# The expert loop of a hybrid S5/SSD/MoE block: scatter and gather moved ahead of each expert's branch

## The chip, the core and the metric

The kernel runs on one core of one Trainium2 chip. The metric is the device time of one execution in microseconds (us); the kernel before takes 1868.61 us, the median of 3 runs (1868.11 to 1870.3). A core has five engines that run side by side, each with an instruction queue of its own: TensorE (PE, matrix products; its weight loads are a row of their own, PEld), VectorE (DVE), ScalarE (ACT), GpSimd (POOL) and SyncE (SP, which here only issues the loads of weights). Weights come from HBM by DMA, through 16 DMA engines.

## What is computed

The reference is one layer: a modulated RMS norm, a projection, an S5 mixer and an SSD mixer, a merge, and then a mixture of experts, which is the second half of the time and all that the change touches. For 256 tokens of width 1024 it is, cut to its core:

```python
logits = (xf @ p['router_w'] + p['router_b']).astype(jnp.float32)
top_val, top_idx = lax.top_k(logits, TOP_K)            # 4 of 32 experts per token
gates = jax.nn.softmax(top_val, axis=-1)
...
def expert_block(args):
    tokens, e = args
    xb = x_pad[tokens]
    gate = jnp.minimum(xb @ p['moe_w_gate'][e] + p['moe_b_gate'][e], SWIGLU_LIMIT)
    up = jnp.clip(xb @ p['moe_w_up'][e] + p['moe_b_up'][e], -SWIGLU_LIMIT, SWIGLU_LIMIT)
    act = (up + 1.0) * gate * jax.nn.sigmoid(SWIGLU_ALPHA * gate)
    return act @ p['moe_w_down'][e] + p['moe_b_down'][e]
...
y = y.reshape(n_slots, d) * slot_gate[:, None].astype(y.dtype)
return jax.ops.segment_sum(y, slot_token, num_segments=n + 1)[:n].reshape(b_, l, d)
```

All weights are float32: three matrices of 1024 x 1024 per expert, 12 MB, for 32 experts.

## The kernel before

**The expert loop** (line 1711) walks experts 0 to 31 in pairs: an even one (j = 0) and the odd one behind it (j = 1). Each expert has room for 64 tokens (CAP). A pair shares one 128-column gather, one slot table and one result tile.

**One expert, in program order.** `load.until` (L1774) issues on SP the loads of weight tiles of 1 MB, four each for gate, up and down. `count` (L1694) reads the expert's token count into registers of PE, ACT and DVE. `before.scale` (L1595) multiplies the last expert's result by its gates on DVE. `inner` does the gate and the up product on PE (both L1502), and `swiglu` (L1506 to L1510) on DVE and ACT, which ends in tile `au`. `beyond` (L1677) is a branch that PE, ACT and DVE take when the expert has more than 64 tokens: it runs a second, smaller pass over the same three weight matrices. The branch bounds the scheduling: no instruction crosses it. Behind it stand, for an even expert, the scatter of the last pair (`scatter`, L1601 on PE and L1603 on DVE: four matmuls of 128x512, each added to `h2`), for an odd one the gather of the next pair (`Pair`, 48 matmuls at L1532, two copies at L1535, one-hot tables at L1518). Then comes `outer`: four transposes of `au` (L1575), their copy `aT` (L1577), for an even expert the pair's slot table (`slots`, L1545 to L1554), and the down product (L1588). The last expert has four warming matmuls (L305) behind its branch.

**What sets the order.** The order on each engine inside a stretch between two branches is chosen by a scheduler. In the profile the end of a branch is line L1681 on the engine's queue (PEq, DVEq); it is there whether or not the branch was taken.

**Buffers.** There are 17 weight tiles of 1 MB (`NBW = 12, 5`), 12 for one expert. The second pass reads gate and up again, so their eight tiles come free only when PE has passed the branch; the four of down come free as the down product reads them. SP's loads go round eight semaphores, so a load also waits until the one eight places before it has landed.

```python
    for e in range(NE):
        this = pair
        load.until(e + 1, sum(NBW))
        ...
        behind = this.inner(e % 2)
        beyond(e, n, levels, T)
        ...
        this.outer(e % 2)
```

Of the kernel before, what the change touches and what calls it, by code (L numbers as in the profile page):

```python
# [49 lines left out]
def build(tc, I, out):  # L50
# [1262 lines left out]
    M = es.enter_context(tc.tile_pool(name="moe", bufs=1, reuse_waits="tile"))  # L1313
    experts.more = es.enter_context(tc.tile_pool(name="moew2", bufs=NBW[1], reuse_waits="tile"))
    moe(tc, I, out, M, ident, epsc, gf, h2, xp, iot, posm, pos3, gate, cnt, first, oneh, bst, experts, warm)
    es.close()

# [163 lines left out]
def moe(tc, I, out, M, ident, epsc, gf, h2, xp, iot, posm, pos3, gate, cnt, first, oneh, bst, load, warm):  # L1481
# [5 lines left out]
    def pst(tag, bufs):  # L1487
        return ps.tile([P, 512], F32, tag=tag, name="p_" + tag, bufs=bufs)
# [23 lines left out]
    class Pair:  # L1512
# [54 lines left out]
            self.u = u_  # L1567
            return mm, *swiglu(pg, pu, g_, s_, u_)

        def outer(self, j):  # L1570
            e = self.e0 + j
            u_ = self.u
            pa = pst("t", 2)
            for q in range(4):
                pe.transpose(pa[:, q * P:(q + 1) * P], u_[:, q * P:(q + 1) * P], ident)  # L1575
            aT = M.tile([P, 4, 2, CAP], F32, tag="aT", name="aT")
            act.copy(aT.rearrange("p a b s -> p (a b s)"), pa)  # L1577
            if j == 0:
                self.slots()
            py = pst("y", 2)  # L1580

            for q in range(2):
                pe.matmul(py[64 * q:64 * q + 64], oneh[:, e:e + 1].to_broadcast([96, CAP]), bst[2][:, 512 * (q ^ j):512 * (q ^ j) + 512],
                          start=True, stop=False)
            for k in range(KD):
                for q in range(2):
                    c = k * D + 512 * (q ^ j)
                    self.done = pe.matmul(py[64 * q:64 * q + 64], aT[:, k % 4, k // 4], wts[e, 2, c // load.unit][:, c % load.unit:c % load.unit + 512],  # L1588
                              start=False, stop=(k == KD - 1))
            self.py = py  # L1590
# [53 lines left out]
    def extra_out(e, c, T):  # L1644

        nq = P // c
        n = D // nq
        nb = n // P
        ST, u_ = T.sb("oST", 256), T.sb("oxu", 512)
        pa = T.ps("t1", "t", 2)  # L1650
        for b in range(nb):
            pe.transpose(pa[:, b * P:(b + 1) * P], u_[:, b * P:(b + 1) * P], ident)
        aT = T.sb("oaT", 512)[:, 0:n]
        act.copy(aT, pa[:, 0:n])
        aT = aT.rearrange("p (b q s) -> p b q s", b=nb, q=nq)
        py = T.ps("t0", "t", 2)
        gemm(py, e, 2, lambda k: aT[:, k % nb, k // nb], c)
        ys = u_[:, 0:n]
        for q in range(nq):
            o = slice(c * q, c * q + c)  # L1660
            dve.tensor_mul(ys[o], py[o, 0:n], gf[o, n * q:n * q + n])
        per = 512 // n
        banks = [T.ps(*b, 2) for b in (("sc0", "sc"), ("sc1", "sc"), ("t1", "t"), ("t0", "t"))]
        for t0 in range(0, 2, per):
            for t in range(t0, t0 + per):
                for q in range(nq):
                    o = slice(c * q, c * q + c)
                    pe.matmul(banks[t0 * nq + q][:, (t - t0) * n:(t - t0 + 1) * n], ST[o, t * P:(t + 1) * P], ys[o], start=True, stop=True)
            for q in range(nq):
                ya = h2[:, t0:t0 + per, n * q:n * q + n]  # L1670
                dve.tensor_add(ya, ya, banks[t0 * nq + q].rearrange("p (t n) -> p t n", t=per))
# [3 lines left out]
    levels = (CAP, 32), (96, 32), (128, 64), (192, 64)  # L1675

    def beyond(e, n, rest, T):  # L1677

        if rest:
            base, c = rest[0]  # L1680
            with tc.If(n > base, label=f"more{e}" if base == CAP and e else None):  # L1681
                extra_in(e, base, c, T)
                extra_out(e, c, T)
                beyond(e, n, rest[1:], T)

    pair = Pair(0)
    last = before = None
    behind = []

    def count(e):  # L1690

        block = nc.cur_bb.bb.instructions
        start = len(block)
        n = nc.values_load(cnt[0:1, e:e + 1], engines=engs, min_val=0, max_val=NTOK)  # L1694
        for ins in block[start:]:
            for b in behind:
                if ins.engine == b.ins.engine:
                    tc.add_manual_dep(ins, b.ins.name, mybir.DependencyInfo(mybir.DependencyClass.NoSync, mybir.DependencyReason.DATA),
                                      reason="order")
        return n  # L1700

    def hint(e, after):

        block = nc.cur_bb.bb.instructions
        start = len(block)
        tc.mark_branch_hint_location(f"more{e}", "LikelyTaken", engines=[ET.PE])
        for ins in block[start:]:
            tc.add_manual_dep(ins, after.ins.name, mybir.DependencyInfo(mybir.DependencyClass.NoSync, mybir.DependencyReason.DATA),
                              reason="order")
# [4 lines that stand above are left out]
        if e == 0:  # L1714
            behind = this.through
        n = count(e)
        T = Shared(M, pst)
        if before:
            before.scale(1 - e % 2)

            hint(e, before.done)
        before = this
        behind = this.inner(e % 2)

        beyond(e, n, levels, T)
        if e % 2 == 0 and last:
            for t in range(2):
                last.scatter(t)
        if e % 2 and e + 1 < NE:
            last, pair = pair, Pair(e + 1)  # L1730
        if e == NE - 1:
            warm(WARM, pst("sc", 2))
        this.outer(e % 2)
    this.scale(1)

    ss = M.tile([P, 2, 2], F32, name="oss")
# [128 lines left out]
```

## Time and profile before

| | before |
|---|---|
| median of 3 runs | 1868.61 us (1868.11 to 1870.3) |
| the profiled execution | 1875.09 us, span 1873.4 us |
| mean granted TensorE clock | 0.934 |
| PE, DVE, ACT busy over the span | 86%, 46%, 25% |
| bytes moved by DMA | 539.54 MB |

The profile is one execution. Times are us from the first instruction; a row of the timeline gives the start, the duration and the instruction, and in brackets how long the engine sat idle before it and who ended that. A matmul of float32 operands shows as two passes in the trace. The expert loop starts near 864 us and holds the rest of the span. Experts 17 and 29 have more than 64 tokens and take the branch once.

### The profile page before, as it was taken

The numbers are of one execution on the slowest core, as the hardware profiler recorded it, in microseconds if no ns is written. First come the engines' busy times: TensorE is split into PE (matmuls) and PEld (weight loads), VectorE is DVE, ScalarE is ACT, GpSimd is POOL, SyncE is SP. The second block draws the span as 40 slices with busy tenths as digits, with TensorE's granted clock in tenths as the row PEclk, the third lists the DMA queues.
The fourth block names the chain that finished last, engine by engine and source line by source line (L and its number), as shares of the span: only waits on it lengthen the run. The fifth ranks groups of instructions, "written<-read, shape, count | busy, mean of one in ns | idle before, by whom it ended". The sixth has DMA issues, their size and how long they took to land. (4 is left out here: it accounts for less than half of the span.)

```text
span 1873.4 us, 28065 instructions
## 1 busy us (share of the span) xinstructions
PE 1616.0 (86%) x11244; PEld 1090.9 (58%) x11244; DVE 869.6 (46%) x1614; ACT 460.2 (25%) x796; POOL 291.1 (16%) x299
## 2 busy tenths in 40 slices
PE   5788888976978799797988989899898998989887
PEld 3566666764766698684555555445445554555443
DVE  6767799888997546754122221222122122221222
ACT  5333453542525565242000000000000000000001
POOL 5133435535432331200000000000000000000000
PEclk8899899888987899897999999999999999999999
DMA  8578545344532357684999999999978999999873
GB/s 300 174 235 239 172 140 140 114 123 113 151 114 63 112 184 264 208 273 188 420 419 421 419 420 419 419 419 420 420 319 366 409 419 419 419 420 420 366 317 146
DMA packets 141458, 539.54 MB, mean 288 GB/s; under 512 B 31752, under 2 KB 44968, under 8 KB 91968
## 3 DMA queue, kind: packets, MB, share of 16 engines
q1 hardware_dynamic: 136032, 526.95, 74.3%
q10 hardware_dynamic: 4656, 8.21, 1.3%
q8 instruction: 138, 2.26, 0.5%
q0 software_dynamic: 560, 1.52, 0.3%
q14 instruction: 72, 0.59, 0.1%
HBM read 529.86 MB, written 6.77 MB: 286 GB/s over the span
## 5 line engine op out<-in xcount | busy, mean ns | idle before, releaser
L1502 PE MATMUL p_gu<-mw,xe 128*64 128x512 f32 x2048 | 475.0, 594 | 5.2 <-DMA mw<-in_mg 3.9
L1502 PEld LDWEIGHTS p_gu<-mw,xe 128*64 128x64 f32 x2048 | 261.9, 137 | 181.6 <-issue 46.5
L1430 PE MATMUL mm<-uh,h 128*128 128x256 f32 (+1 forms) x1152 | 327.9, 364 | 44.5 <-DVE cv L1430 32.0
L1430 PEld LDWEIGHTS mm<-uh,h 128*128 128x128 f32 x1152 | 213.5, 205 | 84.2 <-issue 44.9
L1588 PE MATMUL p_y<-mw,aT 128*64 128x512 f32 x1024 | 236.4, 604 | 0.7 <-ACT aT L1577 0.7
L1430 PE MATMUL mm<-ul,h 128*128 128x256 f32 (+1 forms) x576 | 205.5, 357 | 0.0
L1430 POOL TENSOR_TENSOR h<-w,h 128x512 fp32r<-128x512 f32 x99 | 147.3, 1492 | 285.5 <-ACT h L1430 228.7
L1595 DVE SCALAR_TENSOR_TENSOR ye<-p_y,gs,xq 64x512 f32<-64x512 f32 x64 | 48.0, 750 | 256.8 <-PE p_y L1588 256.3
L1588 PEld LDWEIGHTS p_y<-mw,aT 128*64 128x64 f32 x1024 | 96.2, 139 | 118.5 <-issue 79.5
L1507 ACT ACTIVATE as<-ag 128x512 f32<-128x512 f32 (+1 forms) x34 | 21.0, 617 | 496.3 <-DVE ag L1506 496.3
L1430 ACT CAST h<-w 128x512 fp32r<-128x512 f32 x144 | 88.2, 618 | 164.6 <-PE mm L1430 118.7
L1430 PEld LDWEIGHTS mm<-ul,h 128*128 128x128 f32 x576 | 118.1, 205 | 13.4 <-issue 3.0
L1508 DVE TENSOR_SCALAR au<-p_gu 128x512 f32<-128x512 f32 x32 | 22.1, 692 | 205.7 <-PE p_gu L1502 205.7
L1506 DVE TENSOR_SCALAR ag<-p_gu 128x512 f32<-128x512 f32 (+1 forms) x34 | 23.0, 676 | 185.7 <-PE p_gu L1502 110.4
L1601 PE MATMUL p_sc<-ye,ST 128*128 128x512 f32 x128 | 69.3, 684 | 39.7 <-DVEq L1681 38.8
L1430 DVE SCALAR_TENSOR_TENSOR cv<-mm,cw,cv 128x508 f32<-128x508 f32 (+3 forms) x128 | 85.6, 673 | 12.4 <-ACT cv L1430 12.1
L1532 PE MATMUL p_t<-Sb,xp 128*128 128x128 bf16 x480 | 52.9, 250 | 36.0 <-DVEq L1681 36.0
L355 DVE TENSOR_TENSOR low<-w,hi 128x512 fp32r<-128x512 f32 x80 | 63.4, 800 | 34.9 <-ACT hi L353 34.0
L1430 ACT ACT_TABLE_LOAD x55 | 70.6, 1283 | 32.1 <-DVE cv L1430 31.3
L1601 PEld LDWEIGHTS p_sc<-ye,ST 128*128 128x128 f32 x128 | 23.5, 207 | 85.4 <-issue 62.4
L1577 ACT COPY aT<-p_t 128x512 f32<-128x512 f32 x32 | 18.7, 585 | 221.5 <-PE p_t L1575 221.5
L1532 PEld LDWEIGHTS <-xp 128*128 128x128 bf16 x512 | 43.0, 116 | 48.7 <-issue 40.4
(427 smaller groups left out, 2352.0 us busy)
## 6 DMA issues: line engine op xcount, KB each, us to landing
mw<-in_mg SPq DMA_DIRECT2D x128, 1024.0 KB
mw<-in_mu SPq DMA_DIRECT2D x128, 1024.0 KB
mw<-in_md SPq DMA_DIRECT2D x128, 1024.0 KB
w<-in_wg SPq DMA_DIRECT2D x96, 256.0 KB
ada<-in_ada SPq DMA_DIRECT2D x32, 256.0 KB
Toe<-in_ada SPq DMA_DIRECT2D x16, 512.0 KB
vT<-Ed SPq DMA_DIRECT2D x16, 512.0 KB
l8a<-in_ada SPq DMA_DIRECT2D x16, 512.0 KB
```

Source lines behind the costliest of these rows:

```text
L355: lo.tensor_tensor(low, w, hi.bitcast(F32), op=ALU.subtract)
L1430: return fn(*args, **kw)
L1502: mm = pe.matmul(dst[c * q:c * q + c, 0:n], lhs(k), w[:, o:o + n], start=False, stop=(k == KD - 1))
L1506: dve.tensor_scalar(g_, pg, 7.0, None, op0=ALU.min)
L1507: sg = act.activation(s_, g_, AF.Sigmoid, scale=1.702)
L1508: dve.tensor_scalar(u_, pu, -7.0, 7.0, op0=ALU.max, op1=ALU.min)
L1532: mm = pe.matmul(pt[:, k * P:(k + 1) * P], x[:, t, (k0 + k) * P:(k0 + k + 1) * P], Sb[:, t].rearrange("p j s -> p (j s)"), start=(n == 0), ...
L1577: act.copy(aT.rearrange("p a b s -> p (a b s)"), pa)
L1588: self.done = pe.matmul(py[64 * q:64 * q + 64], aT[:, k % 4, k // 4], wts[e, 2, c // load.unit][:, c % load.unit:c % load.unit + 512], sta ...
L1595: dve.scalar_tensor_tensor(self.y[rows, nh], self.py[rows], self.gs[rows, nh, j:j + 1], gf[rows, 512 * nh:512 * nh + 512], op0=ALU.mult, o ...
L1601: pe.matmul(pc, self.ST[:, nh, t], self.y[:, nh], start=True, stop=True)
```

## The change

The four steps behind the branch are spread around it. For an even expert, `scatter(0)` (the first two of the four matmuls of the last pair's scatter) is written ahead of the branch, and `scatter(1)` (the other two) moves into `outer`, behind the transposes and the slot table. For an odd expert, the whole gather of the next pair is written ahead of the branch. The last expert's warming matmuls are written ahead of its branch too. Nothing is computed that was not before, and nothing is left out.

```diff
-        def outer(self, j):
+        def outer(self, j, other=None):
...
             if j == 0:
                 self.slots()
+            if other:
+                other.scatter(1)
             py = pst("y", 2)
...
-        beyond(e, n, levels, T)
         if e % 2 == 0 and last:
-            for t in range(2):
-                last.scatter(t)
+            last.scatter(0)
         if e % 2 and e + 1 < NE:
             last, pair = pair, Pair(e + 1)
         if e == NE - 1:
             warm(WARM, pst("sc", 2))
-        this.outer(e % 2)
+
+        beyond(e, n, levels, T)
+        this.outer(e % 2, last if e % 2 == 0 else None)
```

What the scheduler makes of it on PE, around the branch of the even expert 30 (`mw,xe` are gate and up, `ye,ST` the scatter, `mw,aT` down). Before, the stretch ends in the up product, and all four matmuls of the scatter stand first behind the branch:

```order
L1502 MATMUL p_gu<-mw,xe 64x512 x4
L1694 TENSOR_LOAD cnt
L1694 ISA x2
L1681 COMPARE_AND_BRANCH
...
L1681 UNCONDITIONAL_BRANCH x5
L1601 MATMUL p_sc<-ye,ST 128x512 x4
L1575 MATMUL p_t<-ident,au 128x128 x4
L1545 MATMUL p_t<-ident,S 128x128 x4
...
L1551 MATMUL p_t<-gate,S 128x2 x4
L1588 MATMUL p_y<-mw,aT 64x512 x16
```

And now, at the same place:

```order
L1603 MATMUL p_sc<-ye,ST 128x512
L1502 MATMUL p_gu<-mw,xe 64x512 x4
L1603 MATMUL p_sc<-ye,ST 128x512
L1502 MATMUL p_gu<-mw,xe 64x512 x4
...
L1683 COMPARE_AND_BRANCH
...
L1683 UNCONDITIONAL_BRANCH x5
L1575 MATMUL p_t<-ident,au 128x128 x4
L1545 MATMUL p_t<-ident,S 128x128 x4
L1551 MATMUL p_t<-gate,S 128x2 x4
L1603 MATMUL p_sc<-ye,ST 128x512 x2
L1590 MATMUL p_y<-mw,aT 64x512 x16
```

The two early scatter matmuls do not stand between the up product and the branch: the scheduler has put them inside the up product, between its weight tiles (four matmuls each). What stands between the up product and the transposes is nothing but the branch.

On PE around the branch of the odd expert 29 (`Sb,xp` and `Sb,xq` are the gather). Before, the up product ends, the branch follows, and the gather's 48 matmuls are first behind it:

```order
L1502 MATMUL p_gu<-mw,xe 64x512 x16
L1694 TENSOR_LOAD cnt
...
L1681 COMPARE_AND_BRANCH
...
L1681 UNCONDITIONAL_BRANCH x5
L1532 LDWEIGHTS xp
L1532 MATMUL p_t<-Sb,xp 128x128
```

And now:

```order
L1532 MATMUL p_t<-Sb,xq 128x128
L1696 TENSOR_LOAD cnt
...
L1683 COMPARE_AND_BRANCH
...
L1683 UNCONDITIONAL_BRANCH x5
L1575 MATMUL p_t<-ident,au 128x128 x4
```

The gather now ends just ahead of the branch: 11 of its matmuls stand ahead of the up product's last four, 37 behind them. The transposes are first behind the branch.

On DVE around the branch of the odd expert 17, whose pair still builds a one-hot table `Sb` for a later gather. Before:

```order
L1510 TENSOR_TENSOR au<-au,as 128x512
L1694 TENSOR_LOAD cnt
L1681 COMPARE_AND_BRANCH
L1614 TENSOR_SCALAR oS<-iot,posm 128x32 x2
...
L1681 UNCONDITIONAL_BRANCH x5
L1518 TENSOR_TENSOR Sb<-iot,pos_8798 128x256
```

And now:

```order
L1510 TENSOR_TENSOR au<-au,as 128x512
L1518 TENSOR_TENSOR Sb<-iot,pos_8798 128x256
L1696 TENSOR_LOAD cnt
L1683 COMPARE_AND_BRANCH
L1616 TENSOR_SCALAR oS<-iot,posm 128x32 x2
```

The table moved ahead of the branch, behind the last step of swiglu; it overwrites the table that the gather reads. Experts 27 and later build none. The last expert's four warming matmuls moved, on PE, from the first place behind its branch to the last place ahead of it.

## Rows read from the trace of the kernel before

**Rows 1.** The page: busy tenths and GB/s in 40 slices of 46.8 us.
```profile
PE   5788888976978799797988989899898998989887
DMA  8578545344532357684999999999978999999873
GB/s 300 174 235 239 172 140 140 114 123 113 151 114 63 112 184 264 208 273 188 420 419 421 419 420 419 419 419 420 420 319 366 409 419 419 419 420 420 366 317 146
```
**Rows 2.** Waits of PE, 880 to 1873 us: total us, times, longest.
```profile
PE p_sc L1601 <- DVEq L1681: 38.8, 15, 2.7
PE p_t L1532 <- DVEq L1681: 36.0, 15, 2.5
...
PE p_gu L1502 <- DMA mw<-in_mg: 3.9, 1, 3.9
```
**Rows 3.** Timeline of PE, DVE and ACT, experts 15 and 16: start, duration, instruction, idle before.
```profile
1321.80 0.69 DVE L1508 TENSOR_SCALAR au<-p_gu 128x512 f32<-128x512 f32 x1 [6.32 <-PE p_gu L1502]
...
1324.40 0.38 PE L1532 MATMUL p_t<-Sb,xp 128*128 128x128 bf16 x4 [2.42 <-DVEq L1681]
...
1327.07 0.61 PE L1575 MATMUL p_t<-ident,au 128*128 128x128 f32 x4
...
1327.77 0.58 ACT L1577 COPY aT<-p_t 128x512 f32<-128x512 f32 x1
1331.90 1.11 PE L1502 MATMUL p_gu<-mw,xe 128*64 128x512 f32 x1 [3.89 <-DMA mw<-in_mg]
...
1353.92 1.94 PE L1502 MATMUL p_gu<-mw,xe 128*64 128x512 f32 x8
```
**Rows 4.** Timeline of SP: the first of four loads, time over the four issues.
```profile
1371.68 7.77 SPq L1774 DMA_DIRECT2D mw<-in_mg  x4
1381.62 29.75 SPq L1774 DMA_DIRECT2D mw<-in_mu  x4
1411.46 2.04 SPq L1774 DMA_DIRECT2D mw<-in_md  x4
...
1504.37 7.83 SPq L1774 DMA_DIRECT2D mw<-in_mg  x4
...
1717.84 7.83 SPq L1774 DMA_DIRECT2D mw<-in_mg  x4
```
**Rows 5.** Timeline of DVE and PE, experts 17 and 18, around the taken branch.
```profile
1385.62 0.69 DVE L1508 TENSOR_SCALAR au<-p_gu 128x512 f32<-128x512 f32 x1 [6.32 <-PE p_gu L1502]
...
1388.04 0.76 PE L1623 MATMUL p_t<-xp,oS 128*32 128x256 bf16 x16 [2.03 <-DVE oS L1614]
...
1438.65 0.69 DVE L1508 TENSOR_SCALAR au<-p_gu 128x512 f32<-128x512 f32 x1 [6.56 <-PE p_gu L1502]
```
**Rows 6.** One stage of 20 us: PE, PEld, DVE, ACT, POOL busy, clock, DMA share, GB/s.
```profile
1460.00:1480.00 20.00, 17.57 (x122) 11.56 (x120) 3.19 (x5) 2.30 (x4) 0.00 (x0) 1.00 0.97 393
```
**Rows 7.** Timeline of DVE and PE, experts 28 to 31.
```profile
1735.19 0.69 DVE L1508 TENSOR_SCALAR au<-p_gu 128x512 f32<-128x512 f32 x1 [6.56 <-PE p_gu L1502]
...
1765.11 0.69 DVE L1508 TENSOR_SCALAR au<-p_gu 128x512 f32<-128x512 f32 x1 [6.32 <-PE p_gu L1502]
...
1788.51 0.59 PE L1532 MATMUL p_t<-Sb,xp 128*128 128x128 bf16 x4 [2.31 <-DVEq L1681]
...
1792.46 0.61 PE L1575 MATMUL p_t<-ident,au 128*128 128x128 f32 x4
1794.10 7.03 PE L1588 MATMUL p_y<-mw,aT 128*64 128x512 f32 x32
...
1817.11 5.37 PE L1601 MATMUL p_sc<-ye,ST 128*128 128x512 f32 x8 [2.66 <-DVEq L1681]
...
1822.32 0.60 PE L1575 MATMUL p_t<-ident,au 128*128 128x128 f32 x4
...
1848.54 3.07 PE L305 MATMUL p_sc<-triUL,ident 128*128 128x256 f32 x8 [2.65 <-DVEq L1681]
1851.40 1.06 PE L1575 MATMUL p_t<-ident,au 128*128 128x128 f32 x4
```

## The prediction

> **What bounds the kernel now.** I read the page's slices first, then PE's waits, then the timeline around single branches, then SP's own timeline. In the slices [rows 1] the expert loop is the right half: the DMA engines are full and move 419 to 420 GB/s, and PE is busy 8 to 9 tenths as well. Two dents stand in the stream of weights, slices 30 to 32 (319, 366, 409 GB/s) and 38 to 39 (366, 317); they follow the two taken branches, of experts 17 and 29. Behind the second one the stream has ended before the program does (146 GB/s in the last slice). So two limits lie close together, and the question for any saving on PE is whether it is ahead of the stream or behind it.
>
> PE's waits [rows 2] answer half of it: its large waits are for the end of the branch on DVE, 38.8 us in 15 scatters and 36.0 us in 15 gathers, 2.4 to 2.6 us each. For weights it waited once for long, 3.9 us at expert 16. Everywhere else in the loop the weights were there before PE came.
>
> How far ahead they were is read from SP. Loads go round eight semaphores, so the fourth gate load of expert e+1 is issued when the last up tile of expert e has landed. For expert 17 that is 1371.68 + 7.77 - 0.33 (one issue, an estimate from four issues within 2.04) = 1379.1 us [rows 4]; the up product's last tile takes 1.94 us [rows 3], so PE could have been through at 1381.1. It was through at 1385.62, where DVE starts on its result [rows 5]: 4.5 us late. For expert 28 the same sum gives 1717.84 + 7.83 - 0.33 + 1.94 = 1727.3 [rows 4] against 1735.19 [rows 7]: 7.9 late. The stream's pace is (1717.84 - 1504.37) / 7 = 30.5 us per expert [rows 4], PE's (1735.19 - 1438.65) / 10 = 29.65 [rows 5, 7]. So PE catches up 0.85 us per expert, reaches the stream at expert 16 (the wait of 3.9 us), loses it in the branch of expert 17 and has not reached it again at 29. Between the branches, PE's time counts only as far as its lag reaches; behind the branch of 29 PE alone counts.
>
> **The change, part by part.** *Odd experts.* At expert 15 the result of the up product reaches DVE at 1321.80, the gather starts at 1324.40 after 2.42 us of idling, the transposes at 1327.07, the copy aT at 1327.77: 5.97 us in all [rows 3]. 48 gather matmuls took 1327.07 - 1324.40 = 2.67 us. After the change 37 of them (2.06 us) run while swiglu runs, 11 (0.61) ahead of the last up tile. DVE still has to pass the branch, now with the table Sb behind the gather: Sb needs the gather's end (about 2.1), then half a microsecond and the branch's own 0.4 or so; I put the transposes at 3.2 us and aT at 3.9. Saved: 5.97 - 3.9 - 0.61 = 1.4 us per odd expert.
>
> *Even experts.* The scheduler put the two early scatter matmuls inside the up product, not behind it, so the idle stretch of 2.66 us stays. The scatter took 1817.11 to 1822.32, 5.2 us, at expert 30 [rows 7]. Sixteen matmuls of the down product, two side by side, take 7.03 us [rows 7], 0.88 a pair, so I price a full-width one of the same columns at 0.88: four are 3.5 us wherever they stand. Saved: 1.7 us where the scatter ran at the lower clock behind the idle stretch as here, near nothing where it did not. Over odd and even, cold and warm, I take 1.0 us per expert; bounds 0.7 (the odd ones' 1.4, halved) and 1.55 (1.4 and 1.7, halved).
>
> *At expert 17.* With a pace of 28.65 PE sits on the stream well before expert 16, so its up product ends at 1381.1 plus a remainder. I take 1.5 us for that (between 0 and the 4.5 seen, nearer to the former, because the load that PE stood at in expert 16 was the next expert's first gate tile, put ahead of a down product whose weights were there, and in the new order that tile stands behind the down product): 1382.6, a gain of 3.0. In the branch PE's first gathering matmul ran at 1388.04, 2.4 us after the up product, waiting for DVE's oS [rows 5]. Now the gather and Sb stand before oS: I add 1.2 us (bounds 0 and 2.1, the whole gather). The weight tiles come free 1.8 us earlier, and the stream, which SP held from 1381.62 to 1411.46 [rows 4], restarts by as much earlier. The small dent at 1460 to 1480, 393 GB/s instead of 419 [rows 6], is 20 x 26/419 = 1.2 us of the stream; there SP again waits for PE, which is ahead by more than that, and I count it as gone.
>
> *At expert 29.* The stream's up tiles for 28 allow 1727.3; one expert later 1757.8; less 1.8 and 1.2 that is 1754.8, plus the remainder of 1.5: 1756.3. Can PE be there? At expert 18 its lag has shrunk by 3.0 - 1.8 = 1.2 from the branch and by the gather that no longer follows it, and ten experts at 1.0 us make 10, against a lag of 7.9: yes, with some to spare. Before, it was 1765.11 [rows 7]. Gain: 8.8 us.
>
> *From there to the end* nothing but PE counts, and each saving is kept. Expert 29: the gather behind the branch (1788.51 to 1792.46 [rows 7]) goes, 3.95 us, less 0.2 for its end reaching into the branch: 3.7. Expert 30: 5.2 us of scatter go, 3.5 come back at two places: 1.7. Expert 31: the warming matmuls, 1851.40 - 1848.54 = 2.9 us [rows 7], move under the swiglu for which PE idles 2.65: 2.9. Together 8.3 us. The load of the final norm's weights on ACT moves ahead of the branch with the gather's copies; PE waited for no load behind 29, so I count it at nothing; uncovered, it costs its 0.5 MB at 419 GB/s, 1.2 us.
>
> *Releases.* Gate and up tiles come free on PE at the branch, which now lies about 2.1 us later behind the up product of an odd expert. While PE is on the stream SP has its queue full eight deep, and I cost it at nothing; the slower rival prices it.
>
> Sum: 8.8 + 8.3 = 17.1 us off the profiled execution's 1875.09. The runs' median is 1868.61, 0.35% lower; I scale and take 17 off: 1851 us, 0.9%.
>
> **The rivals.** *The stream alone* (A). If the stream is the limit up to expert 29 in the timed runs, or PE does not catch up, only the last part stays: 1868.6 - 8.3 = 1860 us. For it: the DMA engines are full in nearly every slice [rows 1]. Against it: the lags of 4.5 and 7.9 us. The Trainium skill (Perfetto Trace Analysis, Identifying the Most-Contended Engine) says to improve the most contended engine; by that rule DMA is it, and PE's gaps up to the last load would be worth nothing. The trace agrees only in part: once, at expert 16, did PE stand for weights.
>
> *A colder clock* (B). PE on the stream stands and starts again, as at expert 16, where the first pass behind the 3.89 us took 1.11 us [rows 3] and PE was 4.5 us late an expert later [rows 4, 5]. If it stays that late at 17 and 29, then 17 gains nothing, the stream is not earlier (1.2 lost in the branch, 1.2 won at the dent), and 29 ends at 1757.8 + 4.5 = 1762.3, a gain of 2.8: with 8.3 that is 11, so 1857 to 1858 us. The Trainium skill (TensorE: Matmul & The Clock Gate, HAM oscillation — how this bites in real kernels) tells that matmuls waiting for each tile's load fall back to the low clock each time; this case shows one such stand.
>
> *Later releases, slower* (C). Where SP waits for the branch, 2.1 us later per odd expert can become 2.1 us of an empty stream. The price: it decides once it exceeds what the end gains, 8.3 us, that is from four odd experts on; with all seven from 17 to 29 it is 14.7 - 8.3 = 6.4 us, 1875 us. For it: the dent at 1460, where the stream ran dry in just this way. Against it: one such dent in a whole loop, and a PE that comes to each branch earlier.
>
> *The savings fall back* (D). If the transposes wait as long as before, because the branch's end on DVE is what they wait for [rows 2] and DVE got more to do ahead of it, little is left but the warming: 1868.6 - 2.9 = 1866 us.
>
> **How the numbers follow.** Forecast 0.60, A 0.17, B 0.13, C 0.05, D 0.05. The forecast's own range: both remainders and the delay in the branch at zero give 17: 4.5, so 29 ends at 1757.8 - 4.5 - 1.2 = 1752.1, a gain of 13.0, with 8.3 that is 21.3, and if the end gains 1.5 more at expert 30 and 31, 1846; the other end is B. The range for 8 in 10 takes in A: 1845 to 1861. What a measurement of this kernel can tell from no change is about 0.2%, 3.7 us: faster by more holds for the forecast, A and B, with a little off for savings that A lacks too: 0.88; within it D and that little: 0.06; slower: C and what I do not see, 0.06.
>
> **What would show it.** In the changed profile: gathers without an idle stretch ahead of them; transposes of odd experts some 3 us behind the up product; the waits of even ones unchanged at 2.6 us, now at the transposes; several waits of PE for weights between experts 5 and 16 and before 29; the up product of 17 through near 1382.6, that of 29 near 1756, the end some 100 us behind it instead of 108.3. It is wrong if the up product of 29 ends near 1765 (A) or the stream shows new dents behind odd experts (C).

## The result, and the profile after

The changed kernel takes 1887.07 us (median of 4, 1884.36 to 1898.81) against 1869.23 of the kernel before: 1.0108 times as long, 95% interval 1.0065 to 1.0151. The forecast was 1851, a gain of 17; it is a loss of 18. The profiled execution took 1886.49 us, its span is 1884.8.

The part ahead of the expert loop differs from execution to execution (DVE starts on expert 0's up product at 879.1 us in the profile of before, at 872.0 in that of after), so the two traces are compared by stages of the loop. A stage ends where DVE starts on an up product's result (`au`, as in [rows 7]). Each trace is one execution (that of before took 1875.09 us, some 6 above its median), so a stage is good to a few us only:

```
us between the au of expert      0-17  17-18  18-29  29-30  30-31  31-end    sum
before                          506.5   53.0  326.5   49.4   31.4    27.5  994.3
after                           518.1   51.5  330.1   58.1   30.8    24.2 1012.8
```

Some 12 us are lost ahead of expert 17, the first with a second pass, 4 between the two such experts and 9 at the second one; the rest wins 5 back. The page's slices of after, PE and GB/s as in [rows 1]:

```profile
PE   5898887876968798788999999999989999999887
...
GB/s 303 193 238 211 178 144 125 129 130 123 135 107 69 116 216 263 228 253 240 398 388 381 415 419 418 419 420 419 419 274 409 401 418 419 420 417 419 326 313 135
```

PE is busier than before; the stream of weights has new dents at the loop's start (398, 388, 381, 415, where before it stood at 419 to 421). The stages of 20 us that hold the largest (columns as in [rows 6]; the last lies in the branch of expert 29):

```profile
900.00:920.00 20.00, 19.21 (x127) 12.38 (x125) 4.00 (x6) 1.76 (x3) 0.00 (x0) 1.00 0.92 368
960.00:980.00 20.00, 16.05 (x99) 7.00 (x99) 2.45 (x4) 1.76 (x3) 0.00 (x0) 0.83 0.85 342
1020.00:1040.00 20.00, 19.04 (x127) 7.96 (x125) 3.14 (x5) 2.39 (x4) 0.00 (x0) 1.00 0.87 335
...
1780.00:1800.00 20.00, 16.84 (x227) 9.02 (x227) 4.04 (x10) 1.91 (x5) 0.00 (x0) 0.89 0.05 18
```

A stage at g GB/s has lost 20 x (419 - g)/419 us of stream: 2.4, 3.7 and 4.0 us in the first three, behind the odd experts 1, 3 and 5; with 0.8 between them (403 GB/s) 10.9 us. From 1760 to 1840 us the same sum is 22.5 us, where before it was 17.4. The two differences make 16 of the 18.5 us.

Why did the weights stop? SP's loads, as in [rows 4]:

```profile
1374.48 7.79 SPq L1776 DMA_DIRECT2D mw<-in_mg  x4
1384.42 30.87 SPq L1776 DMA_DIRECT2D mw<-in_mu  x4
...
1765.91 35.85 SPq L1776 DMA_DIRECT2D mw<-in_mu  x4
```

SP stands before a load until PE frees a tile at the branch; in the last row, at the branch of 29, the four issues spread over 35.85 us (before, over 26.77). PE's waits, 880 to 1885 us, as in [rows 2]:

```profile
PE p_t L1575 <- DVEq L1683: 48.3, 26, 2.7
PE p_t L1575 <- PEq L1683: 9.9, 4, 3.9
PE p_t L1625 <- issue: 5.1, 1, 5.1
```

The 75 us at the branch have become 48, but two kinds of wait are new: the transposes wait for PE's own sequencer at the branch (PEq, 9.9 us at experts 3, 4, 11 and 25), and inside the branch of expert 29 PE stands 5.1 us for nothing that the profile shows. PE waits for no weights at all any more. The branch of the odd expert 3 on PE:

```profile
965.02 0.41 PE L1585 MATMUL p_y<-bst,oneh 96*64 96x512 bf16 x2
969.37 1.09 PE L1575 MATMUL p_t<-ident,au 128*128 128x128 f32 x4 [3.94 <-PEq L1683]
...
971.20 9.24 PE L1590 MATMUL p_y<-mw,aT 128*64 128x512 f32 x32
```

The gather is done, DVE is done (its last step of swiglu ends at 965.18, the table `Sb` at 965.55), and PE does nothing for 3.94 us; the down product behind it starts at the lower clock, 9.24 us instead of 7.09. What went on meanwhile stands in the DMA queues of 965.5 to 969.3 us (packets, MB, share of the engines' time):

```profile
q1 hardware_dynamic: 92, 0.59, 37.5%
q8 instruction: 1, 0.02, 1.8%
q14 instruction: 1, 0.01, 0.5%
```

One packet of queue 8, 16 KiB of instructions. The queue is taken for TensorE's: without the hints that the kernel gives to TensorE alone (e10 below) 28 such waits stand, each with a packet of queue 8 just ahead of its end; the 8 KiB of queue 14 moved at this one stall only. By the trace's DMA records the packet of queue 8 moved from 966.60 to 967.71; PE's next matmul started 1.66 us later. That holds for every new wait:

```
expert   PE stands (us)   packet of instructions   PE goes on   behind the packet
3        3.94 (PEq)       966.60 to 967.71         969.37       1.66
4        3.21 (PEq)       997.38 to 998.40         1000.23      1.83
11       1.25 (PEq)       1209.72 to 1210.81       1212.52      1.71
25       1.51 (PEq)       1653.09 to 1654.11       1656.01      1.90
29       5.13 (issue)     1777.60 to 1778.62       1780.18      1.56
```

The kernel before fetched at expert 3 too: a packet moved there from 966.37 to 967.39, and its gather started at 969.41 behind the usual 2.42 us of waiting for DVE. A fetch lay under the idle stretch. The Trainium skill (Runtime: NRT & Kernel Launch, Instruction fetch mechanics) says that a taken branch whose target page isn't loaded waits for its fetch; the trace agrees and adds the price, 3.94 and 3.21 us at experts 3 and 4, less at 11 and 25, where the gather still ran when the packet started. Taken means here that TensorE jumps, at these four experts over the code of the second pass. At expert 29, which runs that code, the wait of 5.13 us stands inside it.

Experts 15 and 16 of after, against [rows 3]:

```profile
1329.33 0.69 DVE L1508 TENSOR_SCALAR au<-p_gu 128x512 f32<-128x512 f32 x1 [7.20 <-PE p_gu L1502]
...
1332.56 0.63 PE L1575 MATMUL p_t<-ident,au 128*128 128x128 f32 x4 [0.78 <-DVEq L1683]
...
1333.28 0.59 ACT L1577 COPY aT<-p_t 128x512 f32<-128x512 f32 x1 [1.21 <-PE p_t L1575]
...
1350.37 1.12 PE L1603 MATMUL p_sc<-ye,ST 128*128 128x512 f32 x2
...
1353.29 1.13 PE L1603 MATMUL p_sc<-ye,ST 128*128 128x512 f32 x2
...
1358.27 0.69 DVE L1508 TENSOR_SCALAR au<-p_gu 128x512 f32<-128x512 f32 x1 [3.12 <-PE p_gu L1502]
...
1360.89 0.73 PE L1575 MATMUL p_t<-ident,au 128*128 128x128 f32 x4 [2.67 <-DVEq L1683]
```

The odd expert's copy aT comes 3.95 us behind `au`, not 5.97: the gather's idle is gone. But the next up product now holds two scatter matmuls of 1.1 us each, and the even expert's idle is still 2.67 us. What follows such an idle stretch, at expert 12, and under it that stage of 20 us, whose granted clock is the 0.83 ahead of the DMA share:

```profile
1240.02 0.63 PE L1575 MATMUL p_t<-ident,au 128*128 128x128 f32 x4 [2.46 <-DVEq L1683]
...
1241.37 1.50 PE L1551 MATMUL p_t<-gate,S 128*128 128x2 f32 x8 [0.29 <-ACT aT L1577]
1242.73 3.76 PE L1603 MATMUL p_sc<-ye,ST 128*128 128x512 f32 x4
...
1246.42 8.16 PE L1590 MATMUL p_y<-mw,aT 128*64 128x512 f32 x32
```

```profile
1240.00:1260.00 20.00, 19.69 (x80) 7.88 (x82) 3.50 (x6) 1.17 (x2) 0.00 (x0) 0.83 1.01 422
```

The second half of the scatter, four passes, takes 3.76 us here and 3.3 to 3.8 at all 15 even experts. Before, all eight passes took 3.86 us at ten of them, as at expert 16, and 5.37 at five, the cold case of [rows 7]:

```profile
1358.31 3.86 PE L1601 MATMUL p_sc<-ye,ST 128*128 128x512 f32 x8 [2.45 <-DVEq L1681]
```

The second half stands just where PE runs at 1.2 instead of 2.4 GHz (from 1243 to 1246 us the granted clock is 0.50).

Experts 28 to 31, against [rows 7]:

```profile
1739.44 0.69 DVE L1508 TENSOR_SCALAR au<-p_gu 128x512 f32<-128x512 f32 x1 [3.13 <-PE p_gu L1502]
...
1771.71 0.69 DVE L1508 TENSOR_SCALAR au<-p_gu 128x512 f32<-128x512 f32 x1 [7.19 <-PE p_gu L1502]
...
1780.18 0.40 PE L1625 MATMUL p_t<-xq,oS 128*32 128x256 bf16 x2 [5.13 <-issue]
...
1803.84 9.34 PE L1590 MATMUL p_y<-mw,aT 128*64 128x512 f32 x32
...
1829.81 0.69 DVE L1508 TENSOR_SCALAR au<-p_gu 128x512 f32<-128x512 f32 x1 [3.13 <-PE p_gu L1502]
...
1860.62 0.69 DVE L1508 TENSOR_SCALAR au<-p_gu 128x512 f32<-128x512 f32 x1 [6.32 <-PE p_gu L1502]
...
1863.23 0.63 PE L1575 MATMUL p_t<-ident,au 128*128 128x128 f32 x4 [0.73 <-DVEq L1683]
```

The last expert's transposes come 2.6 us behind `au`, before 5.5: the warming matmuls hide as forecast. Expert 29 pays for its 5.13 us and for a lower clock: its down product takes 9.34 us, before 7.03 [rows 7].

### The profile page after: what moved, and what is told of

Its sections match the earlier page's. It is cut to its first block, busy times and chain, and to the rows that moved or that the text cites. A ratio compares the mean times of both kernels' runs of the same rounds, so it can differ in the third digit from the quotient of the medians.

```text
span 1884.8 us, 28052 instructions
## 1 busy us (share of the span) xinstructions
PE 1638.5 (87%) x11244; PEld 944.3 (50%) x11244; DVE 874.6 (46%) x1614; ACT 463.3 (25%) x796; POOL 294.2 (16%) x299
## 5 line engine op out<-in xcount | busy, mean ns | idle before, releaser
L1502 PE MATMUL p_gu<-mw,xe 128*64 128x512 f32 x2048 | 466.2, 596 | 0.0
L1430 PE MATMUL mm<-uh,h 128*128 128x256 f32 (+1 forms) x1152 | 322.2, 359 | 45.5 <-DVE cv L1430 32.1
L1502 PEld LDWEIGHTS p_gu<-mw,xe 128*64 128x64 f32 x2048 | 154.4, 137 | 276.3 <-issue 254.6
L1430 PEld LDWEIGHTS mm<-uh,h 128*128 128x128 f32 x1152 | 209.5, 201 | 85.1 <-issue 41.7
L1590 PE MATMUL p_y<-mw,aT 128*64 128x512 f32 x1024 | 242.7, 627 | 2.7 <-ACT aT L1577 2.7
L1590 PEld LDWEIGHTS p_y<-mw,aT 128*64 128x64 f32 x1024 | 76.1, 146 | 170.0 <-issue 138.2
L1603 PE MATMUL p_sc<-ye,ST 128*128 128x512 f32 x128 | 92.0, 838 | 0.9 <-DVE ye L1597 0.9
L1605 DVE TENSOR_TENSOR h<-h,p_sc 128x512 f32<-128x512 f32 x64 | 44.0, 688 | 103.2 <-PE p_sc L1603 103.1
L1430 ACT ACT_TABLE_LOAD x55 | 70.6, 1283 | 30.4 <-DVE cv L1430 29.6
L1575 PE MATMUL p_t<-ident,au 128*128 128x128 f32 x128 | 22.5, 303 | 61.5 <-DVEq L1683 51.2
L353 ACT CAST hi<-w 128x512 fp32r<-128x512 f32 x80 | 49.1, 620 | 72.2 <-PE mm L345 31.0
```

What stands on the lines that cost most here:

```text
L353: act.copy(hi, w)
L1430: return fn(*args, **kw)
L1502: mm = pe.matmul(dst[c * q:c * q + c, 0:n], lhs(k), w[:, o:o + n], start=False, stop=(k == KD - 1))
L1603: pe.matmul(pc, self.ST[:, nh, t], self.y[:, nh], start=True, stop=True)
L1605: dve.tensor_add(ya, ya, pc)
```

## The experiments

Theory S: the scatter's pieces cost more than they save. Theory R: the gather ahead of the branch delays releases. Theory F (from the traces above): TensorE's fetch behind the branch is no longer covered. All ratios are to the kernel before, with 95% intervals.

**Which part.** The gather alone:

```diff
+        if e % 2 and e + 1 < NE:
+            last, pair = pair, Pair(e + 1)
         beyond(e, n, levels, T)
         if e % 2 == 0 and last:
...
-        if e % 2 and e + 1 < NE:
-            last, pair = pair, Pair(e + 1)
```

> Only the next pair's gather stands ahead of the branch; the scatter (whole) and the last warm run stand behind it as before. Theory S (the loss is the scatter's: its first half was drawn into the up product, so the even experts' idle stayed, and its second half runs at the slow clock): the odd experts' idle ahead of the transposes falls from 2.42 to about 0.8 us, the even ones keep 2.5 us followed by a scatter of 3.9 us, and the time is at or below the kernel before, 1858 to 1869 us. Theory R (the loss is the gather's: it delays the release of an odd expert's gate and up tiles, and PE's sequencer stalls at the branch): the stream keeps the dents at 900 to 920, 960 to 980 and 1020 to 1040 us, waits on PEq at the branch stay (some 10 us over four experts), and the time is 1878 to 1890 us.

1875.6 us, 1.0045 [1.0028, 1.0063]: 8 us slower than before, between the theories. PEq waits 4.7 us at two experts, 4.6 us stalled in expert 29's branch. Odd steps (`au` to the next `au`) are 26.5 us undisturbed (without a stall or a wait for weights), 27.9 before: the forecast's 1.4 us. PE now waits for weights 9.4 us in all, and only one early dent stays, 2.0 us, behind expert 1. Nothing stalls there. The same dent stands in the changed kernel (2.4), in e3, e11 and e15, which also have the gather ahead of the branch, and neither before nor in e2 and e4: this part of the loss is the gather's, as Theory R has it.

The split alone (`outer(e % 2, last ...)` and `scatter(0)` as in the change, gather and warming as before):

> Only the scatter is split, one half ahead of the branch and one behind the transposes; gather and warm run stand behind the branch as before. Theory S: the even idle of 2.5 us stays, the second half takes about 3.8 us for two matmuls, the time is 1878 to 1890 us. Theory R: no new dents in the stream and no PEq waits, the time is 1862 to 1870 us, as before or a little below.

1866.7 us, 0.9998 [0.9979, 1.0018]. No stall. But this is not the changed kernel's order: only the first of the two early matmuls was drawn into the up product; the second stands behind its last tile and fills part of the idle, which is only 1.48 us, and behind that the second half takes 1.96 us, not 3.76 (at 13 of the 15 even experts). So S is not tested as I put it, and the changed kernel's scatter without the gather was not run:

```profile
1287.91 1.94 PE L1502 MATMUL p_gu<-mw,xe 128*64 128x512 f32 x8
1289.78 1.12 PE L1603 MATMUL p_sc<-ye,ST 128*128 128x512 f32 x2
...
1292.72 0.63 PE L1575 MATMUL p_t<-ident,au 128*128 128x128 f32 x4 [1.48 <-DVEq L1683]
...
1294.99 1.96 PE L1603 MATMUL p_sc<-ye,ST 128*128 128x512 f32 x4
```

**Held in place.** In the next two, every TensorE instruction of the moved work gets an order-only dependence on the up product's last matmul, so that the scheduler can't draw it into the up product:

```diff
+    def after_up(f):
+        block = nc.cur_bb.bb.instructions
+        start = len(block)
+        r = f()
+        for ins in block[start:]:
+            if ins.engine == ET.PE:
+                tc.add_manual_dep(ins, behind[0].ins.name, mybir.DependencyInfo(mybir.DependencyClass.NoSync, mybir.DependencyReason.DATA),
+                                  reason="order")
+        return r
...
+            after_up(lambda: [last.scatter(t) for t in range(2)])
...
+            last, pair = pair, after_up(lambda: Pair(e + 1))
...
+            after_up(lambda: warm(WARM, pst("sc", 2)))
         beyond(e, n, levels, T)
```

> Gather, the whole scatter and the last warm run stand ahead of the branch, and their first matmuls are held behind the last matmul of the up product, so that none is drawn into it. Theory S: the even idle is filled (the scatter's four matmuls take 3.9 us between up product and transposes, idle there below 0.5 us), the clock stays at 2.4 GHz, and the time is 1843 to 1860 us, faster than both kernels. Theory R: the gather still delays the release and PE's sequencer still stalls; dents and PEq waits stay, the time is 1868 to 1885 us.

1872.07 us, 1.003 [1.0012, 1.0049]: in R's range, not in S's. PE is faster, 26.5 and 29.4 us per step where undisturbed, and stands longer than in the changed kernel: PEq 13.2 us, issue 13.1 us. Yet it is 15 us below it. In the up product of expert 15 PE stands before single weight tiles, 2.5 us apart:

```profile
1319.54 1.94 PE L1502 MATMUL p_gu<-mw,xe 128*64 128x512 f32 x8 [0.34 <-DMA mw<-in_mu]
1322.04 1.94 PE L1502 MATMUL p_gu<-mw,xe 128*64 128x512 f32 x8 [0.56 <-DMA mw<-in_mu]
```

So a quick PE is not paid for, but it forgives stalls. Only the scatter, held so (gather and warming as before):

> Only the whole scatter stands ahead of the branch, held behind the up product's last matmul; gather and warm run stand behind the branch as before. Theory S: the even idle of 2.5 us is gone, each even expert is 2.0 to 2.5 us shorter, the odd ones are as before; PE then meets the weight stream earlier, so the time falls by less than 15 x 2.3 us: 1850 to 1864 us. Theory R: even releases are 3.9 us later, which dents the stream behind the even experts, 1868 to 1880 us.

1870.37 us, 1.001 [0.9993, 1.0027]: in R's range too. Even steps are only 0.4 to 0.5 us shorter (29.2 to 31.1 us undisturbed, 29.7 to 31.5 before), not 2.0 to 2.5: 0.9 to 1.1 us of idle stay, and at ten of the 15 even experts the down product behind it takes 8.4 to 9.6 us, before 7.1.

**The fetch.** The jump made shorter, `levels = ((CAP, 32),)`, in the changed kernel, in the kernel before, and in e3's:

> The changed kernel with only the first of the branch's four nested levels (room for 32 more tokens; the three deeper levels, which no expert takes on these inputs, are left out), so that the code that a skipped branch jumps over is about a third as long on TensorE's queue. Theory F (the new loss is TensorE's instruction fetch behind the branch, which the idle time hid before): the waits on PEq at the branch (9.9 us over four experts) and the 5.1 us stall inside expert 29's branch go, and with them the stream's dents at 966, 1000 and 1031 to 1040 us; 1870 to 1878 us. Theory S (the scatter's pieces cost more than they save: 3.8 us for the second half, slow clock, idle of the even experts unfilled): nothing of that depends on the jump's length, 1883 to 1890 us.

> The kernel before with only the first level of the branch (the three deeper ones, which no expert takes here, are left out): the control for the run above. Theory F: the fetch behind the branch lay under the idle of 2.4 us that every expert had there, so the time stays within 3 us of the kernel before, 1864 to 1870 us. Theory S says the same. If this one is faster by 8 us or more, fewer instructions are a gain of their own and the run above has to be read against it.

> The kernel of e3 (gather, whole scatter and last warm run ahead of the branch, held behind the up product) with one level of the branch. Theory F: its PEq waits (13.2 us) and issue stalls (5.9, 4.9 and 2.1 us) go; PE then runs into the weight stream at once, and what is gained are the stream's early dents (some 7 us) and part of the one behind expert 29: 1856 to 1865 us, faster than both kernels. Rival (stream alone: PE's time is worth nothing here): 1869 to 1875 us as before.

1889.21 us (1.01 [1.0066, 1.0134]), 1859.58 (0.9956 [0.9938, 0.9975]) and 1859.63 (0.9954 [0.9932, 0.9976]). A miss for F as I put it: the first time is the one S gave, and the waits did not go, they moved (PEq 11.9 us at experts 5, 15 and 27; 19.0 us in the pinned kernel). The control gained 8 us by itself, which is not explained here. The profile of e3's kernel taken once more (its label says one level by mistake; it has all four):

> A second profile of the kernel of e3 (all three ahead of the branch and held behind the up product). Theory F: the stalls come from where the code lies, so they stand at the same experts as in e3: PEq waits of 4.3 us at expert 3, 5.1 at expert 4 and 3.8 at expert 18, and issue waits behind expert 10's transposes and in expert 29's branch. Rival (chance, the state of the DMA queues): other experts, other lengths.

The same experts, 3, 4 and 18, for 4.29, 5.29 and 3.40 us, and 5.05 in expert 29's branch: the stalls belong to the code's layout. Of loop time the two executions of this one kernel differ by 6.7 us (996.5 and 989.9), so one profile's stages are good to a few us only. The kernel tells TensorE ahead of each branch, by a hint, that it is likely to jump, so that the target can be fetched early. The hint moved (`hint(e, this.gated)`, behind the gate product), and removed:

> The changed kernel with the branch's prefetch hint behind the gate product of the same expert (about 8 us ahead of the branch) in place of behind the down product of the expert before (about 16 us ahead). Theory F (TensorE's fetch of the branch's target page is exposed and, as this PE pace has no slack against the weight stream, lost in full): if the later hint keeps the page, the PEq waits (9.9 us) at experts 3, 4, 11 and 25 go and the time falls to 1872 to 1880 us; if the hint has no part in it, the same waits stand at the same experts within 0.3 us, since the code's layout hardly moves, and the time stays at 1883 to 1890 us. Theory S (the scatter's pieces alone): 1883 to 1890 us whatever the PEq waits do.

> The changed kernel without the prefetch hints. Theory F: more branches have to fetch their target when they are reached; each such odd expert waits some 3 to 4 us instead of 0.8, each such even one 3.5 instead of 2.66, in the sum 20 to 50 us more PEq waits and 1900 to 1930 us. If the hints do nothing: PEq waits and time as in the changed kernel, 1883 to 1890 us. Theory S says the latter too.

> The kernel before without the prefetch hints. Theory F with cover (the idle of 2.4 us behind the branch hides most of the 3 us of a fetch): each branch waits 0.5 to 1 us longer than the 2.4 to 2.7 us it waited anyway, 15 to 30 us of PE time in all, part of it swallowed by PE's small lead over the stream: 1875 to 1895 us, a third or less of the 76 us that the same edit cost in the changed kernel. Rival (the hints save the same wherever the gather stands): 1930 us or more.

The later hint: 1888.71 us, 1.0103 [1.0081, 1.0125]; PEq waits as they were (9.8 us), but the stall in expert 29's branch is gone, and its stage 29-30 takes 51.5 us, not 58.1; the gain doesn't show in the time. Without hints the changed kernel takes 1962.96 us (1.0505 [1.0486, 1.0524]), the kernel before 1899.27 (1.016 [1.014, 1.0181]): the same edit costs 76 us in one and 30 in the other, more than I expected of either. PE's waits at the branch without hints, changed kernel first:

```profile
PE p_t L1575 <- PEq L1683: 92.5, 28, 5.5
```

```profile
PE p_sc L1601 <- PEq L1681: 13.5, 5, 3.2
PE p_t L1532 <- PEq L1681: 11.0, 4, 3.1
```

28 branches stand for the fetch where the gather runs ahead of the branch, 9 (and six "issue" waits) where the idle stretch does. Last, the layout alone, 64 and 144 instructions of padding in a level that never runs:

> The changed kernel with 64 more TensorE instructions in code that is never executed (the deepest level of expert 0's branch): every instruction that runs is the same, but all code of the later experts lies 64 instructions further on. Theory F (exposed fetches are the loss): the PEq and issue waits move to other experts and their sum changes (15 us in the changed kernel); the time changes with it by about as much, stalls between the loop's start and expert 5 or in expert 29 counting in full. Theory S (the scatter drawn into the up product): the time stays at 1883 to 1890 us whatever the waits do.

> As the run above with 144 instructions. Theory F: another set of stalls, the time follows their sum, 1 us per 1 us. Theory S: 1883 to 1890 us.

1893.6 us (1.0138 [1.0101, 1.0176]) and 1898.16 (1.0163 [1.0127, 1.02]). The first moved no stall (4.18, 3.02, 1.50, 1.39 and 4.83 us at the same five experts), so it tests nothing; the second moved them (PEq 11.1, issue 7.9 us), and its time, some 10 us above the changed kernel's, is neither theory's: 4 us more of stalls go with it. No layout without stalls was found, so their share is not shown by taking them away.

**One thing undone.** The changed kernel, with only `after_up(lambda: last.scatter(0))`:

> The changed kernel with one thing undone: the scatter's first half is held behind the up product's last matmul; gather and warm run stay where the scheduler draws them. Theory S: the even experts' idle at the transposes falls from 2.66 to about 1.5 us, the clock stays at 2.4 GHz behind it, even-to-odd steps fall from 31.3 to 29.5 us and odd-to-even ones from 28.3 to 27.3, PE gets ahead of the stream and takes up its stalls: 1866 to 1873 us although the PEq waits stay within 3 us of the changed kernel's 9.9. Theory F: the waits stay, so the time stays, 1882 to 1890 us.

1871.24 us, 1.0011 [0.9993, 1.0028]: 16 us back, with most of the stalls left (of the 9.9 us at the branch 7.4, as the one at expert 4 is gone, and 4.6 in the branch of 29):

```profile
PE p_t L1575 <- DVEq L1683: 34.5, 26, 2.3
PE p_gu L1502 <- DMA mw<-in_mu: 11.0, 28, 0.6
PE p_t L1575 <- PEq L1683: 7.4, 3, 3.9
PE p_t L1625 <- issue: 4.6, 1, 4.6
```

The even idle is 1.54 us. At eight of the 15 even experts the second half is back at 1.96 us, as at expert 20; at the other seven it still takes 3.3 to 3.8, as at expert 28, so the clock is only a part of what came back:

```profile
1495.38 1.98 PE L1603 MATMUL p_sc<-ye,ST 128*128 128x512 f32 x4
1498.90 0.63 PE L1575 MATMUL p_t<-ident,au 128*128 128x128 f32 x4 [1.54 <-DVEq L1683]
...
1501.17 1.96 PE L1603 MATMUL p_sc<-ye,ST 128*128 128x512 f32 x4
...
1736.54 3.76 PE L1603 MATMUL p_sc<-ye,ST 128*128 128x512 f32 x4
```

Gather and warming held too:

> The changed kernel as its source reads: the scatter's first half, the gather and the last warm run are held behind the last matmul of the up product, so that none is drawn into it; the second half stays behind the transposes. Theory S with slack (PE's pace decides because it is at the stream's own 30.0 us per expert): the even experts' idle falls from 2.66 to about 1 us, the clock stays up, the second half takes 1.9 us for two matmuls, an odd-to-even step goes from 28.3 to 26.5 us and an even-to-odd step from 31.3 to 29.5; PE gets slack to take up its fetch stalls: 1866 to 1875 us. Theory F alone: the stalls stay, so the time stays, 1881 to 1890 us.

1867.41 us, 0.9994 [0.9979, 1.0008], with 7.9 us of PEq waits and 5.1 in the branch: as S with slack had it.

**What PE's time is worth.** The kernel before without the scatter of 15 pairs (the three lines with `last.scatter` taken out):

> The kernel before without the scatter of the first 15 pairs (60 matmuls on TensorE and the additions behind them on VectorE are left out, so the output is not the reference's); the idle stretch of the even experts stays. PE saves 3.9 to 5.4 us at 15 experts, 60 to 75 us in all. Theory of the stream (the loop goes at the weights' 30.0 us per expert, so PE time is worth nothing except around the two taken branches and the tail): 1855 to 1864 us, many waits of PE for weights. Rival (PE's time is the bound, as the forecast had it for the stretch up to expert 29): 1820 to 1850 us.

1860.9 us, 0.9951 [0.993, 0.9972]: some 65 us less work on PE (ten scatters of 3.86 us and five of 5.37), 10 us less time. PE waits for weights instead, 18.2 us for gate tiles alone. Between 18 and 29 it takes 322.8 us, where the kernel before takes 326.5.

**Versions meant to beat both.** e3 with the later hint, and the split with the warming held ahead of the last branch:

> The kernel of e3 (gather, whole scatter and warm run ahead of the branch, held behind the up product) with the hint behind the gate product. As in e9 the stall of 4.9 us inside expert 29's branch should go and the PEq waits at experts 3, 4 and 18 stay. Behind expert 29 PE alone counts, so the time falls by about 3 to 5 us against e3: 1863 to 1869 us. Rival (the branch is set by the weights that PE waits for): 1868 to 1873 us.

> The split scatter of e2 (gather behind the branch as before) and the last warm run ahead of the last branch, held behind the up product. No stall is exposed in e2, and the last expert's idle of 2.6 us is filled: from the last up product to the end 24.2 us as in the changed kernel, where the kernel before takes 27.5. Expected 1862 to 1865 us, 2 to 5 us below e2 and the kernel before. Rival: the tail is set by the final loads and norm, then 1866 to 1868 us.

1867.33 us (0.9992 [0.9976, 1.0008]): the stall in the branch of 29 went, 4.7 us below e3, as expected. And 1864.97 us (0.9977 [0.9962, 0.9993]), the only kernel with all four levels that beats both, by 0.2%, and no instruction wait beyond 0.3 us. Its last expert, with the warming under swiglu, needs 24.1 us from `au` to the end:

```profile
1834.30 1.99 PE L305 MATMUL p_sc<-triUL,ident 128*128 128x256 f32 x8
1834.42 0.69 DVE L1508 TENSOR_SCALAR au<-p_gu 128x512 f32<-128x512 f32 x1 [6.32 <-PE p_gu L1502]
...
1837.01 0.63 PE L1575 MATMUL p_t<-ident,au 128*128 128x128 f32 x4 [0.71 <-DVEq L1683]
```

## Why the prediction was wrong

The stages of the loop for the kernels that decide it:

```
us between the au of expert      0-17  17-18  18-29  29-30  30-31  31-end    sum
before                          506.5   53.0  326.5   49.4   31.4    27.5  994.3
after                           518.1   51.5  330.1   58.1   30.8    24.2 1012.8
e1 gather alone                 505.0   52.9  323.3   55.1   31.4    27.6  995.4
e3 all pinned                   506.8   54.3  327.2   54.9   29.2    24.2  996.5
e15 first half pinned           506.8   55.1  326.6   53.8   28.9    24.2  995.4
e16 no scatter                  502.6   51.5  322.8   51.4   27.9    25.9  982.1
```

*The step that failed is PE's pace*, 29.65 to 28.65 us per expert. From `au` of expert 18 to that of 28 it was (1739.44 - 1441.57)/10 = 29.79. Within it, the term that failed is the scatter's, four matmuls at 3.5 us "wherever they stand". The odd experts' 1.4 us was right by itself (e1). The two early matmuls, priced at 0.88, cost 0.9 each (an odd step is 28.3 us, against 26.5 in e1) and ate it in the next up product. The two late ones took 3.3 to 3.8 us instead of 1.76: the idle that I said would stay is followed by the lower clock, and I had moved half a scatter into it. So the four cost 5.1 to 5.6 us, where the kernel before paid 3.86 or 5.37, and the even experts, which I had gaining up to 1.7 us, lost. An even step takes 30.4 to 32.3 us undisturbed, before 29.7 to 31.5.

*A cost was not in the list at all*: the fetch behind the branch. I asked what was late next where the idle goes, and named Sb and the branch on DVE; the instruction fetch that ran under the same 2.4 us was not in the rows I read. It adds 9.9 us at four branches and 5.1 in expert 29's.

*How the two meet.* At the loop's start all 17 tiles are full. From there an expert that takes PE longer than the stream's 30.5 us [rows 4] leaves the stream empty at once, and the stream does not win this back; one that takes less gives a lead that the next stalls can use up. e1 and e3 have stalls (e3 longer ones than the changed kernel, 4.33 and 5.10 us at experts 3 and 4) and a quick PE, 26.5 us in odd steps; by their stages they lose no time up to expert 17. The changed kernel has both stalls and slow steps: experts 2 to 4 take 32.2, 34.1 and 33.7 us, and the stream loses 10.9. e15 undoes one thing, the place of the scatter's first half, and 16 us come back with most stalls kept. That the slow steps would be harmless without stalls is not shown, as e2 has another order. In the branch of 29 the changed kernel, e1, e3, e11, e13 and e15 pay a stall of 4.6 to 5.1 us, and nothing has a lead there; it is gone with the later hint (e9, e18) and in two other layouts (e5, e14).

*What a right pace would have brought* is open. The working took 8.8 us at expert 29 from PE's lag of 7.9. But PE can lead the stream only by the tiles that are in store beyond the expert at work, 17 - 12 = 5, some 12.5 us at 2.5 us each (an estimate from 1 MB at 419 GB/s). The kernel before uses 0.85 us per expert, and reached the end of that at expert 16 (the 3.89 us of [rows 3]). Without any scatter in the loop, stage 18-29 is 3.7 us shorter, 0-17 3.9 and 17-18 1.5: the 8.8 us were about all there was, for 65 us less work. e2 and e12, without stalls, get 5.3 and 7.0 us up to there; two executions of one kernel (e3 and its second profile) differ by 6.1 over the same stretch. Rival A, the rule that PE's gaps are worth nothing beside the stream, was the better reading for savings beyond that lead.

*Releases at nothing* was wrong as well: the new dents stand behind odd experts, the sign I gave for rival C; its price came in at the loop's start, not between 17 and 29. Of the 10.9 us there, the 2.4 behind expert 1 are its alone; its share of the rest is not shown. The lower clock of rival B came too, but behind the even experts' idle and the stalls, not at the stream.

*What held.* aT of an odd expert 3.95 us behind `au` (forecast 3.9), even waits still 2.5 to 2.7 us, the last expert's 2.9 us (3.3 measured). Of the end's 8.3 us only this came: stages 29-30 and 30-31 together have +8.1 instead of -5.4.

*Open.* How the 18 us split between stalls, pace and later releases is not shown, as no run has one without the others at the changed kernel's order; why single branches are missed by their hint is not shown; nor why one level instead of four gains 8 us in the kernel before.

## What to carry to other kernels

Before pricing a saving, ask how much lead the engine may have over the stream that feeds it: here five tiles, after which quicker is worth little, while slower counts from a full store on at once. An idle stretch behind a branch may be hiding an instruction fetch; look for packets of the instruction queue in it before filling it. And check where a scheduler really puts work that is written ahead of a branch: held behind the product, the same moves cost nothing.

## What the runs showed of the hardware

- A fetch of 16 KiB of TensorE's instructions mostly takes 0.9 to 1.4 us beside the weight stream, and the next matmul starts 1.2 to 2.0 us behind it; this fits all 117 waits of over 1 us on PEq or "issue" in the loops of the traces here. Where nothing covers it, one mostly costs 3 to 5.5 us.
- The prefetch hint on 31 branches is worth 76 us where nothing covers the fetch (e10), 30 where 2.4 us of idle do (e17).
- Two scatter matmuls took 3.3 to 3.8 us behind an idle stretch of 2.5 to 3.2 us, at all 15 even experts of the changed kernel. Behind one of 1.5 us they took 1.96 at 13 of 15 in e2 and at 8 of 15 in e15, and 3.3 to 3.8 at the others, so the idle's length alone does not decide it.
